# Copies between partitions by transfers, 128-row splits and a later first softmax in a decoder-layer kernel

## The chip, the cores and the metric

One core of a Trainium2 chip runs the whole layer. The metric is the device time of one execution in microseconds, the median over several runs. A profile of one execution gives the trace; its span runs from the first to the last instruction of the program.

The core has five engines with a queue of instructions each, all worked off in order: TensorE (PE in the profile, its weight loads PEld), VectorE (DVE), ScalarE (ACT), GpSimd (POOL) and SyncE (SP), which here issues all transfers.

## The reference

One decoder layer on x of 512 tokens by 1024 channels, float32. After an RMS norm, one wide projection gives a pooling branch, 16 query heads of 64, keys and values for three attention branches with two groups each, and gates. The pooling branch takes causal means over 2, 4, 8 and 16 tokens. Queries and keys get an RMS norm per head and a rotary embedding. The attention has three branches:

- compressed: keys and values are cut into 31 blocks of 32 tokens with stride 16, a position embedding is added, and each block is flattened and put through a two-layer network (gelu) to one key or value; a softmax over these blocks.
- selected: the top 8 blocks of 64 tokens, which with 512 tokens are all 8, so a causal softmax.
- window: the last 512 tokens, again a causal softmax.

```
blk  = k[:, idx] + pos_emb          # idx: 16 * n + (0..31), n = 0..30
flat = blk of one group, (n, 32 * 64)
k_cmp = gelu(flat @ w1 + b1) @ w2
s_c  = q k_cmp ;  p_c = softmax(where(16 * n + 31 <= t, s_c, -inf)) ;  o_c = p_c v_cmp
o    = g0 * o_c + g1 * o_s + g2 * o_w
```

The gated sum goes through a projection, is merged with the pooling branch by sigmoid gates, projected and added to x. Then a second RMS norm and a feed-forward part: an up projection to 2 x 2752 channels, a causal convolution over three tokens, silu(gate) * value, and a down projection, added to x.

## The kernel before

All activations lie transposed, channels on partitions, in tiles of 128 x 512. Every float32 product is computed as three products: each operand is split into a high part `hi` (a copy that rounds, on ScalarE, line 97) and a remainder `lo = x - hi` (line 100, VectorE or GpSimd), and `mm3` adds hi*hi, lo*hi and hi*lo. So every weight tile and every intermediate costs one ScalarE and one VectorE or GpSimd pass before TensorE can use it.

Weights come through `Ring` (lines 148 to 166): SyncE loads 512 KB into one of two buffers `st` (line 155), two splits of 512 columns turn it into `hi` and `lo` tiles (six of each), and the buffer is free for the next load when both splits have read it.

The stages, in the order of the program text: the first projection with the compressed keys and values and the gates (`kva`); `kv_group(0)` and `(1)` for the keys and values of the other branches; four times `pool_in`; `cmp_in`, `cmp_hid`, `cmp_out` for the compressed blocks, once for keys (i = 0) and once for values (i = 1); four times `q_group`; the attention loop; then the projections and the feed-forward part. The program is written with tile pools; a planner puts the instructions of each engine in an order by priority (the order of the text) and by the time at which its own model holds each to be ready, and it inserts the semaphores. So an instruction may stand well before or behind its place in the text, but on the chip each engine, SyncE too, keeps the planned order and waits when an operand is late.

What the change touches:

- `kcd` (lines 330 to 335): compressed keys (0) and values (1) of each block t of 128 tokens, tokens on partitions, 2 groups of 64. `cmp_in` (line 440) copies each group twice side by side into `dup` (line 450, GpSimd), transposes it on TensorE (line 451), so that partitions 0 to 63 and 64 to 127 hold the same 64 channels, and splits even tokens from the lower and odd tokens from the upper half into `X`, 64 rows at a time (line 457): eight splits for keys and eight for values.
- `kv_group` (line 338): line 311 writes the normalised key twice side by side into `k2`, 256 wide, by a broadcast; two transposes (`kt`) and a split give `KHL`.
- `q_group` (line 357): for each pair of token blocks, four transposes fill a PSUM bank `qt`; for each head half, ScalarE copies 64 rows into `qp` (line 376) and VectorE subtracts and writes the remainder into the other 64 rows of the same tile (line 377), which moves it across partitions. So a query head has its high part in one half of the rows and its low part in the other.
- `cmp_out` (line 486), called for keys and values behind two gate tiles `f_g0` (lines 549 to 552).
- the attention loop (lines 752 to 770): `u` counts 32 units (16 heads by two branches). `scores(u)` multiplies queries with keys, `soft` does maximum and exponential, `values(u - 1)` transposes the probabilities and multiplies with the values. Between them, `slot` lets pieces of gate tiles (`fm`) run on TensorE. The compressed branch is done for four heads at a time by `Cmp`: `score()` (8 products, and VectorE's mask addition `cst`), `soft()` (4 transposes `scq`, softmax), `turn()` (4 transposes back). For the first four heads `score()` and `soft()` stand ahead of `scores(0)` (ORD = 0), and `turn()` behind it.

PSUM is shared: three banks `s` (token products, scores), two banks `t` (transposes), two `g` (tiles of 512 columns), one `o`.

Of the kernel before, what the change touches and what calls it, by code (L numbers as in the profile page):

```python
# [11 lines left out]
F32 = mybir.dt.float32  # L12
F32R = mybir.dt.float32r
BF16 = mybir.dt.bfloat16
AF = mybir.ActivationFunctionType
# [4 lines left out]
P = 128  # L20
# [4 lines left out]
DH = 64  # L25
# [51 lines left out]
def layer(ctx: ExitStack, tc: tile.TileContext, par, masks, xT, w_kva, w_tm, w_fm, w_pl, w_pbr,  # L77
# [5 lines left out]
    def nm(s):  # L83
        cnt[0] += 1
        return f"{s}{cnt[0]}"
# [4 lines left out]
    def r32(ap):  # L90
        return ap.bitcast(F32)
# [193 lines left out]
    def head_norm_rope(ps, n, t, tab, out=None):  # L285

        def sc():
            return pp.tile([P, 4, DH], F32, tag="h1k", name=nm("h"), bufs=HB)  # L290
        x_, y_, z_ = sc(), sc(), sc()
        x_, y_, z_ = x_[:, :n], y_[:, :n], z_[:, :n]
        a.activation(x_, ps, AF.Copy, scale=rstd[:, t:t + 1])
        a.activation(y_, x_, AF.Square)
        ss = pp.tile([P, 4], F32, tag="hss", name=nm("hss"), bufs=4)
        v.tensor_reduce(ss[:, :n], y_, AX.X, ALU.add)
        a.activation(ss[:, :n], ss[:, :n], AF.Sqrt, bias=eps, scale=1.0 / DH)
        for h in range(2):
            s_, d_ = 32 * (1 - h), 32 * h
            g.tensor_tensor(z_[:, :, d_:d_ + 32], x_[:, :, s_:s_ + 32],  # L300
                            tabS[tab][:, t, d_:d_ + 32].unsqueeze(1).to_broadcast([P, n, 32]), ALU.mult)
        v.tensor_tensor(y_, x_, tabC[tab][:, t].unsqueeze(1).to_broadcast([P, n, DH]), ALU.mult)
        v.tensor_tensor(y_, y_, z_, ALU.add)
        rs = pp.tile([P, 4], F32, tag="hrs", name=nm("hrs"), bufs=4)
        v.reciprocal(rs[:, :n], ss[:, :n])
        rb = rs[:, :n].unsqueeze(2).to_broadcast([P, n, DH])
        if out is None:
            v.tensor_tensor(y_, y_, rb, ALU.mult)
            return y_
        o, form = out  # L310
        v.tensor_tensor(o, form(y_), form(rb), ALU.mult)
# [15 lines left out]
    heads = lambda ap: ap.rearrange("p (h d) -> p h d", d=DH)  # L327


    kcd = [[p1.tile([P, 2, DH], F32, name=f"kcd{i}{t}") for t in range(NB)] for i in range(2)]  # L330
    for t, ps in enumerate(kva):
        kr = head_norm_rope(heads(ps[:, 0:128]), 2, t, 1)
        g.tensor_copy(kcd[0][t], kr[:, 0:2])
        a.activation(kcd[1][t], heads(ps[:, 128:256]), AF.Copy, scale=rstd[:, t:t + 1])
        a.activation(gt[:, t], ps[:, 256:304], AF.Copy, scale=nrstd[:, t:t + 1])


    def kv_group(b):
        for t, ps in tok_gemm(tm_weights(b), 256):
            vin = heads(ps[:, 128:256])  # L340
            vh = V2[b][t][:, :, 0:DH]
            a.activation(vh, vin, AF.Copy, scale=rstd[:, t:t + 1])
            v.scalar_tensor_tensor(V2[b][t][:, :, DH:P], vin, rstd[:, t:t + 1], r32(vh), ALU.mult, ALU.subtract)

            k2 = pp.tile([P, 2, 2, DH], F32, tag="kq", name=nm("kd"), bufs=KQ)
            head_norm_rope(heads(ps[:, 0:128]), 2, t, 2 + b,
                           (k2, lambda x: x.unsqueeze(2).to_broadcast([P, 2, 2, DH])))
            tp = bank_t("kt")
            for G in range(2):
                pe.transpose(tp[:, G * P:(G + 1) * P], k2[:, G].rearrange("p a d -> p (a d)"), ident)  # L350
            tt = slice(t * P, (t + 1) * P)
            split(KHL[:, b, 0, :, tt], KHL[:, b, 1, :, tt], tp[:, :2 * P].rearrange("p (G q) -> p G q", q=P))
# [4 lines left out]
    def q_group(gq):  # L357
        qp = [qo.tile([P, 2, S], F32R, tag="qo", name=nm("qp"), bufs=8) for _ in range(2)]
        QP[2 * gq:2 * gq + 2] = qp
        for t, ps in tok_gemm(tm_weights(2 + gq), 256):  # L360


            q2 = pp.tile([P, 2, 2, DH], F32, tag="kq", name=nm("qd"), bufs=KQ)
            head_norm_rope(heads(ps[:, :256]), 4, t, 0,
                           (q2.rearrange("p b a d -> p a b d"),
                            lambda x: x.rearrange("p (a b) d -> p a b d", b=2)))
            if t % 2 == 0:
                tp = bank_t("qt").rearrange("p (b q) -> p b q", b=2)
            o = t % 2 * P
            for b in range(2):  # L370
                pe.transpose(tp[:, b, o:o + P], q2[:, b].rearrange("p a d -> p (a d)"), ident)
            if t % 2:
                tt = slice((t - 1) * P, (t + 1) * P)
                for a_ in range(2):
                    rh, rl = slice(64 * a_, 64 * a_ + 64), slice(64 - 64 * a_, 128 - 64 * a_)
                    a.activation(qp[a_][rh, :, tt], tp[rh], AF.Copy)
                    v.tensor_tensor(qp[a_][rl, :, tt], tp[rh], r32(qp[a_][rh, :, tt]), ALU.subtract)

    def fm_tile(ws, ht, hl_):
        ps = bank_g("fm")  # L380
# [59 lines left out]
    def cmp_in(i):  # L440
        XX = p1.tile([P, 16, 2, 2, 32], F32R, tag="X", name=nm("X"))
        Xs[i] = XX
        X = (XX[:, :, 0], XX[:, :, 1])
        g.memset(r32(XX[:, :, :, 1, 31:32]), 0.0)
        split(X[0][:, :, 0, 31], X[1][:, :, 0, 31], pv("pos")[:, 16 * i:16 * i + 16])
        for G in range(2):
            tp = bank_t("ct")
            for t in range(NB):
                dup = p1.tile([P, 2, DH], F32, tag="dup", name=nm("dup"), bufs=3)
                g.tensor_copy(dup, kcd[i][t][:, G].unsqueeze(1).to_broadcast([P, 2, DH]))  # L450
                pe.transpose(tp[:, t * P:(t + 1) * P], dup.rearrange("p a d -> p (a d)"), ident)
            for lo_ in (0, 64):
                rr = slice(lo_, lo_ + 64)
                for c in range(2):

                    src = tp[rr].rearrange("p (n f b) -> p f n b", f=8, b=2)[:, :, c:c + 31, lo_ // 64]
                    split(X[0][rr, 8 * c:8 * c + 8, G, :31], X[1][rr, 8 * c:8 * c + 8, G, :31], src)

    def cmp_hid(i):
        X = Xs[i]  # L460
# [87 lines left out]
    mp = pool(mid, "mp", side="right")  # L548
    for c in range(NPRE):
        f_g0(c, fm_tile(ring(w_fm[4 + c], P, KC), hh, hl), mp)  # L550
    cmp_out(0)
    cmp_out(1)
    mid.close()


# [194 lines left out]
    fetch(0)  # L750
    pbs = [None] * NU
    for u in range(NU + DEPTH):
        if u == ORD:
            pcs[0].score()
            pcs[0].soft()
        if u < NU:
            pbs[u] = scores(u)
        if u == max(ORD, DEPTH - 1):
            pcs[0].turn()
        w = u - DEPTH  # L760
        if w >= 0:
            values(w, pbs[w], pcs[w // 8])
            nq = w // 8 + 1
            if nq < 4:
                if w % 8 == 4:
                    pcs[nq].score()
                elif w % 8 == 5:
                    pcs[nq].soft()
                elif w % 8 == 7:
                    pcs[nq].turn()  # L770
# [195 lines left out]
```

## Time and profile before

| what | value |
|---|---|
| median of 3 runs | 843.5 us (842.94 to 844.76) |
| the profiled execution | 842.97 us |
| its span | 840.9 us |
| TensorE clock granted, mean | 0.994 |
| VectorE, ScalarE, GpSimd busy | 68%, 55%, 28% |
| HBM read | 69.94 MB |

How to read the profile: an engine's busy time is the union of its instructions. An idle stretch ahead of an instruction is given with what released it, in brackets: `[3.24 <-DVE plo L103]` means that the engine stood idle for 3.24 us until VectorE had written `plo` in line 103. PEclk is the granted share of TensorE's full clock. A line number can be a helper's: L97 and L100 are `split`, L109 to L111 `mm3`, L155 the weight load.

### The profile page before, as it was taken

What the parts mean: (1) busy time and instruction counts of PE and PEld (TensorE: products, weight loads), DVE (VectorE), ACT (ScalarE), POOL (GpSimd) and SP (SyncE); (2) the same over time, 40 slices, a digit from 0 to 9 for tenths busy, and PEclk for the clock granted to TensorE, in tenths of its full rate; (3) what the DMA queues carried; (4) which work ended last, traced back from release to release, by engine and by line L of the source; (5) the groups of instructions that cost most, each with busy time, mean ns of one, the idle gap of its engine ahead of it and who ended that gap; (6) DMA issues with size and microseconds to landing.
All of it is one profiled execution on the core that took longest, in us unless ns stands there. A gap on an engine that the chain in (4) does not pass through costs nothing.

```text
span 840.9 us, 12107 instructions
## 1 busy us (share of the span) xinstructions
PE 817.7 (97%) x4291; PEld 696.8 (83%) x4291; DVE 571.4 (68%) x1194; ACT 464.4 (55%) x985; POOL 233.7 (28%) x326
## 2 busy tenths in 40 slices
PE   7999989989999999999999999999999999999998
PEld 6888878968878878788888888888888888888888
DVE  7599976778887888886565438877777777522321
ACT  6755767757787877785334436544554454322220
POOL 5696714347575655642001200000000000000000
PEclk9999989999999999999999999999999999999999
DMA  6333132330100101011443332233332333343430
GB/s 217 103 101 113 51 101 96 107 101 25 51 26 26 51 17 35 27 39 42 135 149 112 101 103 77 101 101 101 100 91 90 97 100 116 92 128 103 113 101 26
DMA packets 23116, 72.82 MB, mean 87 GB/s; under 512 B 2832, under 2 KB 3472, under 8 KB 23056
## 3 DMA queue, kind: packets, MB, share of 16 engines
q1 hardware_dynamic: 23056, 72.05, 27.5%
q8 instruction: 34, 0.56, 0.3%
q14 instruction: 26, 0.21, 0.1%
HBM read 69.94 MB, written 2.10 MB: 86 GB/s over the span
## 4 chain that ended last, share of the span: by engine, by line
PE 85%; DVE 7%; ACT 3%; DMA 2%; issue 1%; POOL 0%; SPq 0%; ACTq 0%; DVEq 0%; POOLq 0%
PE fm L109 16%; PE fm L111 16%; PE fm L110 16%; PE op L729 5%; PE dn L109 5%; PE dn L111 5%; PE dn L110 5%; PE tp L722 4%; PE ss L691 2%; PE ss L692 2%; PE tg L321 2%; PE tg L319 2%; PE tg L320 2%; DMA st<-in_w_fm 1%; PE pb L109 1%
## 5 line engine op out<-in xcount | busy, mean ns | idle before, releaser
L97 ACT ACTIVATE hi<-st 128x512 fp32r<-128x512 f32 (+3 forms) x253 | 152.2, 607 | 189.3 <-PE fm L110 89.6
L100 DVE TENSOR_TENSOR lo<-st,hi 128x512 fp32r<-128x512 f32 (+1 forms) x210 | 145.2, 695 | 100.5 <-ACT hi L97 99.2
L109 PE MATMUL fm<-h2h,hi 128*128 128x512 f32 x344 | 134.0, 389 | 0.0
L110 PE MATMUL fm<-h2l,hi 128*128 128x512 f32 x344 | 133.8, 389 | 0.0
L111 PE MATMUL fm<-h2h,lo 128*128 128x512 f32 x344 | 133.7, 389 | 0.0
L703 POOL TENSOR_TENSOR pb<-pb,sm 128x128 f32<-128x128 f32 (+3 forms) x128 | 91.8, 748 | 49.8 <-DVE sm L700 26.1
L681 ACT ACTIVATE pb<-pb,nm 128x384 f32<-128x384 f32 (+3 forms) x128 | 70.9, 555 | 16.2 <-DVE nm L680 15.4
L111 PEld LDWEIGHTS fm<-h2h,lo 128*128 128x128 f32 x344 | 64.6, 188 | 13.5
L110 PEld LDWEIGHTS fm<-h2l,hi 128*128 128x128 f32 x344 | 64.6, 188 | 13.4
L109 PEld LDWEIGHTS fm<-h2h,hi 128*128 128x128 f32 x344 | 64.6, 188 | 13.2
L109 PE MATMUL fm<-hh,hi 128*128 128x512 f32 x160 | 71.7, 448 | 0.0
L680 DVE CUSTOM_DVE_ANT_0 pb<-ss,mk 128x384 f32<-128x384 f32 (+3 forms) x128 | 58.9, 486 | 16.7 <-PE ss L692 13.2
L110 PE MATMUL dn<-gl,hi 128*128 128x512 f32 (+1 forms) x189 | 69.1, 365 | 0.0
L111 PE MATMUL dn<-gh,lo 128*128 128x512 f32 (+1 forms) x189 | 69.1, 365 | 0.0
L109 PE MATMUL dn<-gh,hi 128*128 128x512 f32 (+1 forms) x189 | 69.1, 365 | 0.0
L111 PE MATMUL fm<-hh,lo 128*128 128x512 f32 x160 | 63.4, 397 | 0.7 <-POOL lo L100 0.7
L100 DVE TENSOR_TENSOR ptl<-tp,pth 128x512 fp32r<-128x512 f32 (+1 forms) x96 | 56.6, 594 | 10.8 <-ACT pth L97 10.2
L110 PE MATMUL fm<-hl,hi 128*128 128x512 f32 x160 | 63.4, 396 | 0.0
L97 ACT ACTIVATE pth<-tp 128x512 fp32r<-128x512 f32 (+1 forms) x96 | 49.3, 517 | 22.8 <-PE tp L722 22.5
L100 POOL TENSOR_TENSOR lo<-st,hi 128x512 fp32r<-128x512 f32 x36 | 47.2, 1313 | 41.6 <-ACT hi L97 35.6
L319 PE MATMUL tg<-hi,hh 128*128 128x256 f32 x192 | 54.4, 286 | 0.0
L320 PE MATMUL tg<-hi,hl 128*128 128x256 f32 x192 | 54.4, 286 | 0.0
(256 smaller groups left out, 1815.9 us busy)
## 6 DMA issues: line engine op xcount, KB each, us to landing
st<-in_w_up SPq DMA_DIRECT2D x43, 512.0 KB, 3.5
st<-in_w_dn SPq DMA_DIRECT2D x24, 448.0 KB, 3.4
st<-in_w_fm SPq DMA_DIRECT2D x20, 512.0 KB, 3.5
st<-in_w_tm SPq DMA_DIRECT2D x12, 512.0 KB, 3.4
st<-in_w_ab SPq DMA_DIRECT2D x8, 512.0 KB, 3.5
st<-in_w_o SPq DMA_DIRECT2D x8, 512.0 KB, 3.4
x<-in_xT SPq DMA_DIRECT2D x15, 256.0 KB, 3.7
st<-in_cw SPq DMA_DIRECT2D x4, 512.0 KB, 3.5
```

What stands on the lines that cost most here:

```text
L97: a.activation(hi, src, AF.Copy)
L100: (eng or v).tensor_tensor(lo, src, r32(hi), ALU.subtract)
L109: pe.matmul(ps, sh, mh_, start=first and i == 0, stop=False)
L110: pe.matmul(ps, sh, ml_, start=False, stop=False)
L111: pe.matmul(ps, sl, mh_, start=False, stop=last and i == n - 1)
L319: pe.matmul(ps[:, :n], hh[k][:, tt], H, start=k == 0, stop=False)
L320: pe.matmul(ps[:, :n], hl[k][:, tt], H, start=False, stop=False)
L680: v.tensor_tensor_reduce(p_, ps, mcaus[:, S - n:], -1.0, 3e38, ALU.add, ALU.min, nm_[:, i:i + 1])
L681: a.activation(p_, p_, AF.Exp, bias=nm_[:, i:i + 1], scale=-1.0, accum_out=sm[:, i:i + 1])
L703: g.tensor_tensor(pb[:, PBASE[i]:PBASE[i] + n], pb[:, PBASE[i]:PBASE[i] + n], sm[:, i:i + 1].to_broadcast([P, n]), ALU.mult)
L722: last = pe.transpose(tp[:, n:n + P], pb[:, PBASE[i] + j * P:PBASE[i] + (j + 1) * P], ident)
L729: pe.matmul(op[:, j * P:], V2[b][j][:, G], pt_[:, TBASE[j]:TBASE[j] + w], start=b == 0 and j == 0 and part == 0, stop=False)
```

## The change

The compressed keys and values go into one tile per i, `kcd[i]`, with room for two copies of each token's 64 channels: the second place of row p is to hold the token of row p + 1. For each of the four token blocks a transfer copies rows 1 to 127 one row up into the second place, and one more transfer fills row 127 from row 0 of the next blocks. GpSimd clears the second place of the last block first. `cmp_in` then transposes `kcd` directly: `dup` is gone, and since the lower half now holds token p and the upper half token p + 1, one split of 128 rows takes the even columns of both, four splits for keys and four for values.

In `kv_group`, line 311 writes `k2` once and ScalarE copies it to the second place. In `q_group` one split of 128 rows fills two new tiles `qs0` (two buffers) and `qs1` (one), and four transfers of 64 rows bring their halves into `qp`. `cmp_out(0)` moves between the two `f_g0` tiles. In the loop, `score()` of the first four heads comes behind `scores(0)`, `soft()` behind `scores(1)` and `turn()` behind `scores(2)`.

```
--- before.py
+++ after.py
@@ -327,12 +327,18 @@
     heads = lambda ap: ap.rearrange("p (h d) -> p h d", d=DH)
 
 
-    kcd = [[p1.tile([P, 2, DH], F32, name=f"kcd{i}{t}") for t in range(NB)] for i in range(2)]
+
+    kcd = [p1.tile([P, NB, 2, 2, DH], F32, name=f"kcd{i}") for i in range(2)]
+    for i in range(2):
+        g.memset(kcd[i][:, NB - 1, :, 1], 0.0)
     for t, ps in enumerate(kva):
-        kr = head_norm_rope(heads(ps[:, 0:128]), 2, t, 1)
-        g.tensor_copy(kcd[0][t], kr[:, 0:2])
-        a.activation(kcd[1][t], heads(ps[:, 128:256]), AF.Copy, scale=rstd[:, t:t + 1])
+        head_norm_rope(heads(ps[:, 0:128]), 2, t, 1, (kcd[0][:, t, :, 0], lambda x: x))
+        a.activation(kcd[1][:, t, :, 0], heads(ps[:, 128:256]), AF.Copy, scale=rstd[:, t:t + 1])
         a.activation(gt[:, t], ps[:, 256:304], AF.Copy, scale=nrstd[:, t:t + 1])
+    for k_ in kcd:
+        for t in range(NB):
+            nc.sync.dma_start(k_[:P - 1, t, :, 1], k_[1:, t, :, 0])
+        nc.sync.dma_start(k_[P - 1:, :NB - 1, :, 1], k_[:1, 1:, :, 0])
 
 
     def kv_group(b):
@@ -343,8 +349,8 @@
             v.scalar_tensor_tensor(V2[b][t][:, :, DH:P], vin, rstd[:, t:t + 1], r32(vh), ALU.mult, ALU.subtract)
 
             k2 = pp.tile([P, 2, 2, DH], F32, tag="kq", name=nm("kd"), bufs=KQ)
-            head_norm_rope(heads(ps[:, 0:128]), 2, t, 2 + b,
-                           (k2, lambda x: x.unsqueeze(2).to_broadcast([P, 2, 2, DH])))
+            head_norm_rope(heads(ps[:, 0:128]), 2, t, 2 + b, (k2[:, :, 0], lambda x: x))
+            a.activation(k2[:, :, 1], k2[:, :, 0], AF.Copy)
             tp = bank_t("kt")
             for G in range(2):
                 pe.transpose(tp[:, G * P:(G + 1) * P], k2[:, G].rearrange("p a d -> p (a d)"), ident)
@@ -371,10 +377,13 @@
                 pe.transpose(tp[:, b, o:o + P], q2[:, b].rearrange("p a d -> p (a d)"), ident)
             if t % 2:
                 tt = slice((t - 1) * P, (t + 1) * P)
+                qs = [pp.tile([P, 2, 2 * P], F32R, tag=f"qs{j}", name=nm("qs"), bufs=2 - j) for j in range(2)]
+                split(qs[0], qs[1], tp)
                 for a_ in range(2):
-                    rh, rl = slice(64 * a_, 64 * a_ + 64), slice(64 - 64 * a_, 128 - 64 * a_)
-                    a.activation(qp[a_][rh, :, tt], tp[rh], AF.Copy)
-                    v.tensor_tensor(qp[a_][rl, :, tt], tp[rh], r32(qp[a_][rh, :, tt]), ALU.subtract)
+                    rh = slice(64 * a_, 64 * a_ + 64)
+                    for j in range(2):
+                        ro = slice(64 * (a_ ^ j), 64 * (a_ ^ j) + 64)
+                        nc.sync.dma_start(r32(qp[a_][ro, :, tt]), r32(qs[j][rh]))
 
     def fm_tile(ws, ht, hl_):
         ps = bank_g("fm")
@@ -446,15 +455,11 @@
         for G in range(2):
             tp = bank_t("ct")
             for t in range(NB):
-                dup = p1.tile([P, 2, DH], F32, tag="dup", name=nm("dup"), bufs=3)
-                g.tensor_copy(dup, kcd[i][t][:, G].unsqueeze(1).to_broadcast([P, 2, DH]))
-                pe.transpose(tp[:, t * P:(t + 1) * P], dup.rearrange("p a d -> p (a d)"), ident)
-            for lo_ in (0, 64):
-                rr = slice(lo_, lo_ + 64)
-                for c in range(2):
-
-                    src = tp[rr].rearrange("p (n f b) -> p f n b", f=8, b=2)[:, :, c:c + 31, lo_ // 64]
-                    split(X[0][rr, 8 * c:8 * c + 8, G, :31], X[1][rr, 8 * c:8 * c + 8, G, :31], src)
+                pe.transpose(tp[:, t * P:(t + 1) * P], kcd[i][:, t, G].rearrange("p a d -> p (a d)"), ident)
+            for c in range(2):
+
+                src = tp.rearrange("p (n f b) -> p f n b", f=8, b=2)[:, :, c:c + 31, 0]
+                split(X[0][:, 8 * c:8 * c + 8, G, :31], X[1][:, 8 * c:8 * c + 8, G, :31], src)
 
     def cmp_hid(i):
         X = Xs[i]
@@ -548,8 +553,7 @@
     mp = pool(mid, "mp", side="right")
     for c in range(NPRE):
         f_g0(c, fm_tile(ring(w_fm[4 + c], P, KC), hh, hl), mp)
-    cmp_out(0)
-    cmp_out(1)
+        cmp_out(c)
     mid.close()
 
 
@@ -750,12 +754,13 @@
     fetch(0)
     pbs = [None] * NU
     for u in range(NU + DEPTH):
-        if u == ORD:
-            pcs[0].score()
-            pcs[0].soft()
         if u < NU:
             pbs[u] = scores(u)
-        if u == max(ORD, DEPTH - 1):
+        if u == 0:
+            pcs[0].score()
+        if u == 1:
+            pcs[0].soft()
+        if u == 2:
             pcs[0].turn()
         w = u - DEPTH
         if w >= 0:
```

## Rows read from the trace of the kernel before

**Rows 1.** The page's busy times: us, share of the span, instructions of each engine.

```profile
PE 817.7 (97%) x4291; PEld 696.8 (83%) x4291; DVE 571.4 (68%) x1194; ACT 464.4 (55%) x985; POOL 233.7 (28%) x326
```

**Rows 2.** Busy time by stretch: length, then each engine, PEclk, DMA share, GB/s.

```profile
60.00:80.00 20.00, 18.20 (x147) 17.48 (x146) 19.24 (x37) 10.70 (x29) 14.94 (x23) 1.00 0.28 79
...
100.00:115.00 15.00, 10.54 (x56) 9.07 (x55) 14.34 (x28) 12.06 (x26) 5.05 (x8) 0.77 0.33 96
115.00:176.00 61.00, 61.00 (x377) 53.97 (x376) 42.81 (x98) 42.60 (x90) 22.08 (x33) 1.00 0.31 98
176.00:187.00 11.00, 7.61 (x33) 6.10 (x33) 7.44 (x19) 5.50 (x15) 2.55 (x2) 0.84 0.33 95
```

**Rows 3.** The same view in windows of 2 us, for PEclk (third number from the end).

```profile
108.00:110.00 2.00, 1.55 (x7) 1.55 (x8) 1.91 (x4) 0.94 (x3) 0.00 (x0) 0.50 0.61 225
112.00:114.00 2.00, 2.00 (x12) 2.00 (x11) 1.94 (x4) 1.75 (x6) 0.15 (x1) 0.53 0.28 43
182.00:184.00 2.00, 2.00 (x9) 1.81 (x10) 1.59 (x8) 0.38 (x2) 0.00 (x0) 0.54 0.45 184
184.00:186.00 2.00, 2.00 (x8) 1.61 (x7) 0.67 (x3) 1.39 (x5) 0.00 (x0) 0.61 0.00 0
```

**Rows 4.** Timeline of PE and DVE: start, length, engine, line, operands, count.

```profile
108.45 0.79 PE L473 MATMUL hp<-hi,X 128*128 128x256 f32 x2 [3.24 <-DVE plo L103]
...
181.15 0.69 DVE L624 TENSOR_TENSOR cst<-sc,mk 128x512 f32<-128x512 f32 x1
...
181.89 0.90 PE L629 MATMUL scq<-pk,cst 128*128 128x128 f32 x4 [3.39 <-DVE cst L624]
```

**Rows 5.** Groups by line and shape: count, busy us, mean ns, idle before (qp: 80 to 115).

```profile
L377 DVE TENSOR_TENSOR qp<-qt,qp 64x512 fp32r<-64x512 f32 x5 | 3.4, 688 | 0.3 <-ACT qp L376 0.2
...
L100 DVE TENSOR_TENSOR X<-ct,X 64x248 fp32r<-64x248 f32 x16 | 6.6, 413 | 4.0 <-ACT X L97 3.8
L311 DVE TENSOR_TENSOR kd<-h,hrs 128x256 f32<-128x256 f32 x8 | 6.0, 760 | 0.1
...
L450 POOL COPY dup<-kcd 128x128 f32<-128x128 f32 x16 | 5.6, 375 | 10.6 <-PE ct L451 10.6
...
L100 DVE TENSOR_TENSOR KHL<-kt,KHL 128x256 fp32r<-128x256 f32 x8 | 3.2, 410 | 0.0
```

**Rows 6.** Timeline of ACT and DVE: first value copy and last key of `kcd`.

```profile
31.36 0.39 ACT L334 ACTIVATE kcd<-raw,rstd 128x128 f32<-128x128 f32 x1
...
45.71 0.29 DVE L308 TENSOR_TENSOR h<-h,hrs 128x128 f32<-128x128 f32 x1
```

**Rows 7.** Transfers of the span: packets; queue's share; issues, KB, us to landing.

```profile
DMA packets 23116, 72.82 MB, mean 87 GB/s; under 512 B 2832, under 2 KB 3472, under 8 KB 23056
...
q1 hardware_dynamic: 23056, 72.05, 27.5%
...
out<-o SPq DMA_DIRECT2D x2, 128.0 KB, 1.9
...
w<-in_cw SPq DMA_DIRECT2D x2, 32.0 KB, 4.2
```

**Rows 8.** Timeline of SyncE's queue: two weight loads, start and length of the issue.

```profile
49.71 0.33 SPq L155 DMA_DIRECT2D st<-in_w_tm  x1
...
106.59 0.33 SPq L155 DMA_DIRECT2D st<-in_w_tm  x1
```

**Rows 9.** Transfers in the window 13.9 to 14.1 us.

```profile
DMA packets 30, 0.01 MB, mean 31 GB/s; under 512 B 30, under 2 KB 30, under 8 KB 30
...
q1 hardware_dynamic: 30, 0.01, 15.2%
```

**Rows 10.** Timeline of PE where `kv_group(1)` begins.

```profile
57.60 0.39 PE L110 MATMUL fm<-hl,hi 128*128 128x512 f32 x1
57.83 0.28 PE L319 MATMUL tg<-hi,hh 128*128 128x256 f32 x1
```

**Rows 11.** Timeline of PE, the first transposes of `cmp_in`.

```profile
87.29 0.49 PE L451 MATMUL ct<-pk,dup 128*128 128x128 f32 x3
```

## The prediction

> **What bounds the kernel now.** Read the page's engine shares first: TensorE is busy for 97% of the span [rows 1]. So time can be won only where TensorE stands idle or runs at the lower of its two clocks, and is lost where a new wait stops it. Next the stretches [rows 2]: from 115 to 176 us TensorE is busy throughout, and three stretches leave something. From 60 to 80 it idles 20.0 - 18.2 = 1.8 us; from 100 to 115, 4.5; from 176 to 187, 3.4. VectorE tells why in the first two: it is busy 19.2 of 20 and 14.3 of 15 us, so TensorE has run ahead of its evictions.
>
> Third, short windows for the clock [rows 3] with the timeline beside them [rows 4]. After the 3.24 us idle before `hp` (line 473) the granted clock is 0.50, the 1.2 GHz level, from 108 until about 113; after the 3.39 us idle before `scq` (line 629) it is about half from 182 to somewhat before 186. Work done at half speed could have been done in half the time, so the dips cost about 4.8/2 = 2.4 and 3.5/2 = 1.75 us. The prize is 4.5 + 2.4 = 6.9 us at 100 to 115 (place A), 3.4 + 1.75 = 5.1 at 176 to 187 (place B), 1.8 at 60 to 80 (place C): 13.8 us at most.
>
> **The change part by part: what it takes away.** First, whether 128 rows cost more than 64. They don't: VectorE's subtraction takes 413 ns on 64x248 (`X`) and 410 on 128x256 (`KHL`) [rows 5]. So half the count is half the time.
>
> `cmp_in`: 16 subtractions of 413 ns become 8, saving 3.3 us of VectorE (half of it before 115 us) and about as much of ScalarE. The 16 `dup` copies at 375 ns leave GpSimd, 6.0 us. `q_group`: 16 subtractions of 688 ns become 8; five of the 16 lie before 115, so 2.5 x 0.69 = 1.7 us goes there. `kv_group`: the multiplication of line 311 becomes 128 wide instead of 256; its eight take a mean of 760 ns against 290 for an undisturbed 128-wide one [rows 5, 6], at best 3.8 us, by the undisturbed 410 ns of a 256-wide operation 1.0; I take 2. ScalarE gets eight 128-wide copies instead, 0.39 us each by the `kcd` row [rows 6]; it has room (10.7 busy of 20 us at 60 to 80 [rows 2]), but every `kt` transpose waits one hop longer.
>
> VectorE thus loses about 1.7 + 1.7 + 2 = 5.4 us of its work before 115, more than the 4.5 us of idle at A. I credit 5 of A's 6.9 us (in-order engines keep a remainder) and all 1.8 of C. Bounds for both: 2.2 (only the two `q_group` and two `cmp_in` subtractions next to the stalled `plo` splits, 2 x 0.69 + 2 x 0.41) and 8.7.
>
> The loop's start: at B, TensorE has issued `sc`, and its next instruction, the `scq` transposes, waits for `cst`, which VectorE reaches only at 181.15, behind older work [rows 4]. After the change `scores(0)` stands ahead of `score()`: its products need only `KHL` and `QP[0]`, and behind each of its four blocks come two pieces of an `fm` tile: 4 x 2 x 3 products of 512 columns, 0.23 us apart [rows 10], 5.5 us of work that waits for nothing on VectorE. That covers the 3.4 us. I credit 4.5 of 5.1 (bounds 3.4 and 5.1): `soft()` and `turn()` now crowd VectorE among the first units. `cmp_out(0)` ahead of `f_g0(1)` I cost at nothing: TensorE is solid there.
>
> Credit: 5 + 1.8 + 4.5 = 11.3 us, bounds 5.6 and 13.8.
>
> **What it adds.** SyncE gets 10 transfers for `kcd` and 32 for `qp`. A `qp` copy is 128 KB; the nearest row lands in 1.9 us [rows 7], and SyncE issues a transfer in 0.33 us, four in 1.3 [rows 8]. Nobody reads `qp` before the attention, and two token blocks lie between pairs, 48 products of 256 columns at half of the 0.23 us that one of 512 takes [rows 10], 5.5 us, so the single `qs1` is free again by then. I take 0.5 us for weight loads that stand behind them; bounds 0 and 9 (second rival).
>
> The `kcd` copies decide. Each of eight moves 127 rows of two pieces of 256 B, 254 pieces. What does a piece cost? The trace holds no copy within the chip, but it holds the loads of `w2`, 128 pieces of 256 B each [rows 7]. In a window in which only such small packets move, 30 of them take 15.2% of 16 engines for 0.2 us: 0.486/30 = 16 ns each [rows 9]. From the other sides: by bytes alone, 72.05 MB in 27.5% of 16 x 840.9 us, 256 B take 13 ns; the mean packet, 12 times larger, takes 160 ns [rows 7]. I take 16, the row of the same size.
>
> How many of the 16 DMA engines share the pieces? In this kernel every transfer has 128 or 64 rows, which divide by 16, and the page shows how they are dealt: of 2832 packets under 512 B [rows 7], 256 are the `w2` rows; the other 2576 are 16 x 161, and 161 is the number of transfers in the list of issues: one closing packet from each engine for each. 127 is prime: it can't be dealt in equal shares to 16 engines, nor to any number but one. So there are two cases: one engine, 254 x 16 ns = 4.1 us a copy, or all sixteen, 0.26 us and nothing to notice. I take one engine, since every share in the trace is an equal one.
>
> The Trainium skill says this outright ("DMA: Bandwidth & Descriptors", section "Why a DMA increments its semaphore by 16 and not by 1"): a hardware-queued transfer runs on the largest number of engines up to 16 that divides the slowest dimension of both its sides, and 127 rows is its example of a transfer that gets one. The 16 closing packets agree for 128 and 64 rows; no run here shows 127. By that rule the sum is the one below, without it the first rival's.
>
> With one engine: the first `kcd[1]` copy is ready at 31.36 + 0.39 = 31.75 (line 334), the last `kcd[0]` one at 46.0 (line 308) [rows 6]. The first can move data from about 31.75 + 1.9 = 33.6 on; the eight follow each other, to 33.6 + 8 x 4.1 = 66.4. Weight loads go out on the same queue in SyncE's order and use all 16 engines, so their sixteenth on that engine waits. Behind the copies come the `w_fm` load of `pool_in(3)` and the first `w_tm` load of `kv_group(1)`, issued at 49.71 [rows 8]; each adds 8 packets of 160 ns, 1.3 us, so the second lands at 69.0. With 0.6 for ScalarE's cast TensorE starts `kv_group(1)` at 69.6 where it started at 57.83 [rows 10]: 11.8 us late, with nothing else to do in its order. The wait comes in two gaps (before `pool_in(3)` and before `kv_group(1)`), each likely over 3 us, so I add the two measured dips, 2.4 + 1.75 = 4.2. Cost 16.0 us. At 13 ns it is 5.6 late with half the dips, about 8; at 20 ns 19.9 and 4.2, about 24. The `ct` transposes, which read the copies, come at 87.29 [rows 11], so that wait is covered; late are the weights behind the copies.
>
> **Sum.** 842.97 (the profiled execution) - 11.3 + 0.5 + 16.0 = 848.2. The runs' median lies 0.5 above the profiled one: 848.7.
>
> **Rivals.** First, faster: the 127 rows are dealt over all engines, or the planner puts the copies behind the weight loads. Then a copy is 2 us of latency that nobody reads before 87 us, and the credit stays: 843.5 - 11.3 + 0.5 = 832.7. For it: SyncE is busy for 0.33 us per load only; against it: the equal shares. It decides from where the eight copies are done before the `w_tm` load of 49.71, at 2 us a copy or less.
>
> Second, no change: without one engine, the transfers' place in SyncE's in-order queue eats the credit. A weight load behind four `qp` copies waits for the split that they wait for (0.7) and for four issues (1.3); another 0.3 for their packets. The load issued at 106.59 [rows 8], just before the `q_group` work at 113, stands so. Four such places, 9.2 us: 842. Against it: the loads wait for the same VectorE anyway.
>
> Third, much slower: a piece within the chip costs 25% more than one from memory, 20 ns, or the queue stops SyncE too: 857 and above.
>
> **How the numbers follow.** Chances: forecast 0.58, first rival 0.27, second 0.08, third 0.07. Within 0.2% (1.7 us) counts as the same, about what a measurement of this kernel tells from no change. The forecast's own range is 840 to 857, from 13 to 20 ns; since its credit and its cost are both larger than their difference, I give 0.42 of its 0.58 to slower, 0.08 to the same, 0.08 to faster. First rival: 0.25 faster, 0.02 the same. Second: 0.03 the same, 0.02 faster, 0.03 slower. Third: slower. Sums: faster 0.35, same 0.13, slower 0.52. The range reaches over the first rival and leaves out a tenth on either side: 831 to 857.
>
> **What would show it.** One engine: fewer than 16 closing packets a transfer, `kcd` copies that land 4 us apart, the `w_tm` load issued near 50 landing late, and a TensorE gap that ends on a weight split between 52 and 70 us. Credit: no gap over 1 us before `hp`, none before `scq`, and a clock of 1.00 there. If TensorE runs through 50 to 70 us as before, the forecast is wrong and the first rival holds; if the gaps at A and B remain, the credit is.

## The result: 1.5 per cent slower, and the profile after

The changed kernel takes 856.66 us (median of 4 runs, 856.32 to 857.26) against 843.43 for the kernel before: ratio 1.0154, 95% interval 1.0142 to 1.0166. That is 13.2 us more, where the forecast's sum has 5.2. The profiled execution has a span of 854.4 us.

The page's own lines, those that answer to [rows 1, 7]:

```profile
PE 820.4 (96%) x4291; PEld 699.4 (82%) x4291; DVE 557.9 (65%) x1178; ACT 456.7 (53%) x977; POOL 226.8 (27%) x308
...
DMA packets 29790, 77.55 MB, mean 91 GB/s; under 512 B 5409, under 2 KB 10145, under 8 KB 29729
...
q1 hardware_dynamic: 29728, 76.77, 30.2%
```

VectorE, ScalarE and GpSimd all do less, 13.5, 7.7 and 6.9 us, and the kernel is slower: their sums say nothing of the end. The stretches do (columns as in [rows 2]):

```profile
40.00:60.00 20.00, 11.49 (x61) 9.25 (x60) 11.12 (x29) 5.06 (x16) 9.89 (x17) 0.87 0.08 16
60.00:80.00 20.00, 13.24 (x58) 11.07 (x59) 11.93 (x23) 8.54 (x22) 10.54 (x13) 0.71 0.42 126
...
100.00:120.00 20.00, 20.00 (x162) 19.42 (x161) 16.73 (x40) 14.02 (x36) 10.35 (x17) 1.00 0.42 107
120.00:140.00 20.00, 17.69 (x88) 14.40 (x87) 13.99 (x36) 12.76 (x29) 2.76 (x5) 0.91 0.65 184
...
208.00:222.00 14.00, 10.34 (x53) 8.24 (x52) 8.67 (x28) 7.21 (x20) 8.87 (x11) 0.88 0.00 1
```

From 40 to 80 us TensorE is busy for 24.7 of 40 us and no other engine for more; such a hole in all of them at once points at a transfer. SyncE's queue (start, us, engine, line, operands, count; lines 340 and 341 are the `kcd` copies, 155 the weight loads) shows which. Before, the last `w_fm` load of the early stages went out like this:

```profile
43.45 0.33 SPq L155 DMA_DIRECT2D st<-in_w_fm  x1
```

In the changed kernel, some lines left out:

```profile
36.38 8.35 SPq L340 DMA_DIRECT2D kcd<-kcd  x2
44.77 4.14 SPq L341 DMA_DIRECT2D kcd<-kcd  x1
48.96 8.36 SPq L340 DMA_DIRECT2D kcd<-kcd  x3
57.42 4.05 SPq L155 DMA_DIRECT2D st<-in_w_fm  x1
...
67.17 1.76 SPq L155 DMA_DIRECT2D st<-in_w_tm  x2
```

An issue of a weight load took 0.33 us before. Of the eleven issues from 32 to 67 us (ten copies and the `w_fm` load), eight hold SyncE for 3.3 to 4.8 us each and three for under 1 us. So the `w_fm` load goes out at 57.42 instead of 43.45, and the `w_tm` load of 49.71 [rows 8] at 67.17. While only copies move, the transfers of the window 40 to 44 us are

```profile
DMA packets 244, 0.06 MB, mean 16 GB/s; under 512 B 244, under 2 KB 244, under 8 KB 244
...
q1 hardware_dynamic: 244, 0.06, 7.9%
```

244 pieces in 4 us are one every 16.4 ns. 7.9% of sixteen engines is 1.3 engines, so by engine time a piece takes 20.7 ns: each begins a little before the one ahead of it is done. ScalarE and TensorE then wait in one chain (timeline; in brackets the idle time before and what ended it):

```profile
65.36 1.15 ACT L97 ACTIVATE hi<-st 128x512 fp32r<-128x512 f32 x2 [15.82 <-DMA st<-in_w_fm]
...
66.76 0.69 PE L356 MATMUL kt<-pk,kd 128*128 128x128 f32 x2 [14.60 <-ACT kd L353]
```

`kt` waits for ScalarE's copy of `kd`, which stands behind the cast of the late weights. So it is one gap of 14.60 us, and the half clock after it (0.50 from 60 to 70, 0.83 from 70 to 75) costs about 2.5 more.

At the loop's start the wait before `scq` [rows 4] is gone, and there is this in the changed kernel:

```profile
210.53 0.17 DVE L643 TENSOR_TENSOR csm<-csm,gt 128x16 f32<-128x16 f32 x1
210.69 2.75 POOL L707 TENSOR_TENSOR pb<-pb,sm 128x128 f32<-128x128 f32 x4 [1.58 <-DVE csm L643]
...
213.40 1.05 POOL L646 TENSOR_TENSOR ce<-ce,csm 128x512 f32<-128x512 f32 x1
...
214.50 0.66 PE L652 MATMUL pct<-pk,ce 128*128 128x128 f32 x4 [3.29 <-POOL ce L646]
```

The `pct` transposes wait for `ce`, which in GpSimd's order stands behind four multiplications of the next unit. 3.29 us and a clock of 0.88 over 14 us: the wait that went, in another place.

Two marks on TensorE divide the 13.5 us by which the two profiled spans differ. The 17th `hp` product, the first of the second `cmp_hid`, starts at 150.04 before and 162.59 after, 12.6 later; the 200th `op` product, well inside the attention, at 346.60 and 360.01, 13.4 later; from there on the distance stays.

### The profile page after: what moved, and what is told of

Its sections match the earlier page's. It is cut to its first block, busy times and chain, and to the rows that moved or that the text cites. A ratio compares the mean times of both kernels' runs of the same rounds, so it can differ in the third digit from the quotient of the medians.

```text
span 854.4 us, 12146 instructions
## 1 busy us (share of the span) xinstructions
PE 820.4 (96%) x4291; PEld 699.4 (82%) x4291; DVE 557.9 (65%) x1178; ACT 456.7 (53%) x977; POOL 226.8 (27%) x308
## 4 chain that ended last, share of the span: by engine, by line
PE 80%; DVE 8%; DMA 4%; ACT 3%; issue 2%; POOL 2%; SPq 1%; DVEq 0%; ACTq 0%; POOLq 0%
PE fm L109 15%; PE fm L111 15%; PE fm L110 15%; PE dn L111 4%; PE dn L109 4%; PE dn L110 4%; PE op L733 4%; PE tp L726 4%; DMA st<-in_w_fm 2%; PE ss L695 2%; PE ss L696 2%; PE tg L321 1%; PE tg L320 1%; PE tg L319 1%; PE pb L109 1%
## 5 line engine op out<-in xcount | busy, mean ns | idle before, releaser
L100 DVE TENSOR_TENSOR lo<-st,hi 128x512 fp32r<-128x512 f32 (+1 forms) x210 | 142.9, 685 | 108.7 <-ACT hi L97 107.8
L685 ACT ACTIVATE pb<-pb,nm 128x384 f32<-128x384 f32 (+3 forms) x128 | 70.9, 555 | 14.2 <-DVE nm L684 13.5
L111 PEld LDWEIGHTS fm<-h2h,lo 128*128 128x128 f32 x344 | 64.6, 188 | 13.5
L109 PEld LDWEIGHTS fm<-h2h,hi 128*128 128x128 f32 x344 | 64.6, 188 | 13.4
```

What stands on the lines that cost most here:

```text
L100: (eng or v).tensor_tensor(lo, src, r32(hi), ALU.subtract)
L109: pe.matmul(ps, sh, mh_, start=first and i == 0, stop=False)
L111: pe.matmul(ps, sl, mh_, start=False, stop=last and i == n - 1)
L685: a.activation(p_, p_, AF.Exp, bias=nm_[:, i:i + 1], scale=-1.0, accum_out=sm[:, i:i + 1])
```

## The experiments

Fifteen kernels; each ratio is to runs of the kernel before on the same chip (medians 843.2 to 843.8), with its 95% interval.

**The copies, dealt over all engines.** In the changed kernel:

```diff
-            nc.sync.dma_start(k_[:P - 1, t, :, 1], k_[1:, t, :, 0])
+            for r0, r1 in ((0, 112), (112, P - 1)):
+                nc.sync.dma_start(k_[r0:r1, t, :, 1], k_[r0 + 1:r1 + 1, t, :, 0])
```

> The changed kernel, but each 127-row copy of kcd is made by two transfers of 112 and 15 rows (16 and 15 equal shares). Theory (127 rows go through one DMA engine, 4.2 us a copy, and hold the weight loads): the 14.6 us gap of TensorE at 52 to 67 us and the half clock behind it go, 856.7 - 16 = 840.5 us (838 to 843), no SyncE issue over 1 us there. Rival (copies within the chip or their number in SyncE's queue are slow however they are dealt): 10 transfers more make it no better, 855 or above.

Measured: 841.70 us, ratio 0.9974 (0.9959 to 0.9989). The same bytes in more transfers take 15.0 us off. TensorE's waits for ScalarE's `kd` (us in total, times, the longest), in the changed kernel and then here:

```profile
PE kt L356 <- ACT kd L353: 15.7, 2, 14.6
```

```profile
PE kt L357 <- ACT kd L354: 2.7, 2, 1.8
```

The gap is gone. Shown: the number of rows in a transfer made it.

**What a copy of n rows takes by itself.** In the kernel before, one copy every second unit of the attention, into a tile that is written only later:

```diff
+    rows = {4 + 2 * i: n for i, n in enumerate((128, 127, 126, 125, 124, 122, 120, 112, 127, 128))}
     for u in range(NU + DEPTH):
...
+        if u in rows:
+            n = rows[u]
+            o = min(1, P - n)
+            nc.sync.dma_start(lad[:n, :, 1], lad[o:o + n, :, 0])
```

> The kernel before, with ten copies within the chip added during the attention, some 24 us apart, each of n rows of two pieces of 256 B that nobody reads; n = 128, 127, 126, 125, 124, 122, 120, 112, 127, 128. If the rows are dealt in equal shares over the largest number of engines up to 16 that divides n (16, 1, 14, 5, 4, 2, 15, 16, 1, 16), then at 16 ns a piece the pieces take 0.26, 4.1, 0.29, 0.8, 1.0, 2.0, 0.26, 0.22, 4.1, 0.26 us beyond a common start of some 2 us. If only odd or prime counts go to one engine, 126, 124, 122 and 120 land alike and as early as 128. If the copies are slow for another reason (the shift by one partition), 126 to 112 land as late as 127. The time of the whole kernel should not change: nobody waits for them.

The planner drew the ten copies together, each issued when the one before had landed. The transfers of five windows, each from one copy's issue to the next one's, for 127, 126, 125, 124 and 112 rows:

```profile
DMA packets 255, 0.07 MB, mean 11 GB/s; under 512 B 255, under 2 KB 255, under 8 KB 255
...
DMA packets 266, 0.06 MB, mean 27 GB/s; under 512 B 266, under 2 KB 266, under 8 KB 266
...
DMA packets 255, 0.06 MB, mean 24 GB/s; under 512 B 255, under 2 KB 255, under 8 KB 255
...
DMA packets 252, 0.06 MB, mean 23 GB/s; under 512 B 252, under 2 KB 252, under 8 KB 252
...
DMA packets 240, 0.06 MB, mean 27 GB/s; under 512 B 240, under 2 KB 240, under 8 KB 240
```

Two pieces a row leave 1, 14, 5, 4 and 16 closing packets, one for each engine that took part: the largest divisor of n up to 16. This is the rule of the Trainium skill ("DMA: Bandwidth & Descriptors", section "Why a DMA increments its semaphore by 16 and not by 1"), and here the trace agrees with it count by count. From issue to issue it is 5.95 and 6.02 us for 127 rows, then 2.36, 2.70, 2.78 and 2.13. One engine has 254 pieces where each of sixteen has 14, and 240 x 16 ns is 3.84, the difference of 127 and 112. The second theory of the expectation falls, since 125 rows, odd, run on five engines; so does the third, since 126 rows are shifted too. The one timed execution, 845.07, lies inside the spread of the kernel before (841.7 to 845.2).

**Who stands: the queue or the engine?** The changed kernel with its ten copies issued by ScalarE:

```diff
-            nc.sync.dma_start(k_[:P - 1, t, :, 1], k_[1:, t, :, 0])
-        nc.sync.dma_start(k_[P - 1:, :NB - 1, :, 1], k_[:1, 1:, :, 0])
+            nc.scalar.dma_start(k_[:P - 1, t, :, 1], k_[1:, t, :, 0])
+        nc.scalar.dma_start(k_[P - 1:, :NB - 1, :, 1], k_[:1, 1:, :, 0])
```

> The changed kernel (856.7 us) with its ten kcd copies, 127 rows as they are, issued by ScalarE's queue instead of SyncE's. If the weight loads were late because SyncE itself stood in its issues, each 4.2 us after the other, they go out in time now: 843 to 846 if ScalarE doesn't stand likewise, and 860 or more if it does (its casts then wait 4 us behind each issue). If they were late because a sixteenth of each lies on the one engine that the copies fill, they stay late: 853 to 857.

Measured: 861.48 us, ratio 1.0217 (1.0203 to 1.0231). ScalarE's timeline in it (ACTq is its queue of transfers):

```profile
36.63 8.34 ACTq L340 DMA_DIRECT2D kcd<-kcd  x2
45.02 0.29 ACT L297 ACTIVATE hss<-hss,eps 128x2 f32<-128x2 f32 x1 [9.79 <-issue]
```

ScalarE computes nothing for 9.79 us, ended by "issue": two issues hold it for 8.34 us, about as long as two copies take. TensorE waits 11.88 us for ScalarE's cast of `hi` (at 52.02). The one DMA engine makes a copy long; the standing issuer carries it to everything behind.

Does a weight load beside such copies also wait for its share on their engine, as the prediction had it? This run can't say, but the ladder's trace can. There a `w_fm` load went out at 199.52, 0.8 us behind the copy of 122 rows, which two engines share. The packets from 202.70 to 203.02 us, then those from 203.70 to 203.80:

```profile
DMA packets 29, 0.06 MB, mean 192 GB/s; under 512 B 14, under 2 KB 14, under 8 KB 29
```

```profile
DMA packets 2, 0.00 MB, mean 0 GB/s; under 512 B 2, under 2 KB 2, under 8 KB 2
```

Fourteen of the load's closing packets come by 203.02, the last two, as many as the copy has engines, some 0.7 us later, and it lands 4.7 us after its issue instead of 3.4. So both happen: the issuer stands, and a load's share waits on the engines that a copy fills. How they divide the gap of 14.60 us is not shown.

**The loop's start, undone, alone, and undone with whole-engine copies.** The edit between the kernels is the last part of the change's diff.

> The changed kernel with the start of the attention loop as before (score and soft ahead of scores(0), turn behind it). Theory (the loop's edit only moved TensorE's wait from scq to pct, 3.4 us against 3.3): 855 us (854 to 857.5), the 3.4 us gap before scq back, no gap before pct. Rival (the edit is worth the 4.5 us that was credited, and something else lost them): 861.

> Both edits: copies of 112 and 15 rows, loop start as before. Theory: the two effects add, 839 to 840 us; what then remains against before (843.4) is the credit of the splits at 100 to 115 us, about 4. Rival (the splits are worth nothing, all of it was the loop's): 843.

> The kernel before with only the new start of the attention's loop (scores(0) first, then score(), soft() after scores(1), turn() after scores(2)). By the forecast's term B: 843.8 - 4.5 = 839.3. By what the changed kernel's trace shows, the wait before scq (3.4 us) goes and one before pct, behind GpSimd's multiplications of scores(1), comes in its place with the half clock after it: 844 to 847. If the new gap only comes with the other edits, 840.

Measured: the changed kernel with the old start 853.49 us, ratio 1.0115 (1.0093 to 1.0136), 3.2 less than with the new one; the same with 112 + 15 rows 839.52, 0.9944 (0.9927 to 0.9961), 2.2 less than the first experiment; the new start alone on the kernel before 845.95, 1.0032 (1.0021 to 1.0043), 2.3 more. Three pairs, one sign: the new order costs 2 to 3 us where a win of 4.5 was forecast. In the first two TensorE waits before `scq` (2.32 and 2.67 us), in the third before `pct`. The second and the third:

```profile
178.12 0.66 PE L634 MATMUL scq<-pk,cst 128*128 128x128 f32 x4 [2.67 <-DVE cst L629]
```

```profile
203.34 0.86 PE L648 MATMUL pct<-pk,ce 128*128 128x128 f32 x4 [3.30 <-POOL ce L642]
```

The marks agree: from the one to the other it is 197.4 us in the changed kernel, 195.3 in the same with the old start, and 196.6 in the kernel before.

**Is it GpSimd's order?** Two edits of the first experiment: `ce` of the first four heads on VectorE, and `soft()` one step earlier, which puts `ce` ahead of the multiplications.

```diff
-            g.tensor_tensor(e, e, smb, ALU.mult)
+            (v if self.h0 == 0 else g).tensor_tensor(e, e, smb, ALU.mult)
```

> Copies of 112 and 15 rows, the changed loop start, and the multiplication of e by the row factors for the first four heads on VectorE instead of GpSimd. Theory (pct waits for ce because ce stands behind four pb multiplications of 2.75 us in GpSimd's order): the 3.3 us gap before pct shrinks under 1 us and its half clock goes, 4 us less than the copies of 112 and 15 rows alone, 836.5 (835 to 838.5). Rival (the softmax chain on VectorE is itself that late): within 1 us of them.

```diff
             pcs[0].score()
-        if u == 1:
             pcs[0].soft()
```

> As the first run (copies in 112 + 15 rows, the changed loop, 841.7 us), but soft() is called right after score(), one step earlier: GpSimd's multiplication ce then stands ahead of the four of scores(1) instead of behind them, and scq is the transposes after score() with nothing between. If GpSimd's order makes the pct wait (3.29 us and a dip), it goes: 838 to 839 with a smaller wait before scq (under 2 us, as scores(0) gives VectorE time). If the softmax chain on VectorE is itself the last, the wait stays as in the fourth run or moves to scq: 840.5 to 842.

Measured: 840.56 us, ratio 0.9956 (0.9936 to 0.9976), and 841.84, 0.9976 (0.9963 to 0.9989), against 841.70 without them. My theory of GpSimd's order falls as a cause of the time. In the former the `pct` wait shrinks to 1.15 us and one before `ss` grows from 0.62 to 1.16. In the latter it is gone, and TensorE waits here instead (timeline of that kernel, of the slowest of its twelve executions, which spread from 838.70 to 843.77):

```profile
183.14 0.47 PE L696 MATMUL ss<-KHL,qp 128*128 128x512 f32 x1 [1.39 <-DVE nm L685]
...
189.17 0.33 PE L727 MATMUL tp<-pk,pb 128*128 128x128 f32 x1 [2.11 <-POOL pb L708]
```

Each order names another operand that comes last. So the theory became: what TensorE lacks there is work that waits for nothing.

**Work in place of order.** Eight pieces of an `fm` tile (5.5 us of products) between `score()` and `soft()`, the old order otherwise; the pieces behind are spread a little more thinly. First on the kernel with 112 + 15 rows and the old start, then on the kernel before:

```diff
-            pcs[0].score()
+            slot(8, pcs[0].score())      # score() returns its last product
             pcs[0].soft()
```

> As the third run (112 + 15 rows, the loop's start as before, 839.5 us), with eight pieces of an fm tile (8 x 3 products of 512 columns, 5.5 us) between score() and the scq transposes; the other pieces are spread more thinly over the units behind. If what TensorE lacks at the loop's start is work that waits for nothing, the wait before scq (2.67 us) and its half clock go and nothing comes in their place: 836. If the wait only moves on again, as it did to pct, 839 to 841: the chain of VectorE and GpSimd, not the order, sets the start, or the later units miss their pieces.

> The kernel before with nothing changed but the eight pieces of an fm tile between score() and the scq transposes. If the idle at the loop's start is a prize of its own (the ninth run won 4 us with it on top of the third), 839.5 us, with no wait before scq and none before pct. If the nine run's gain needs the earlier VectorE of the other edits, the wait before scq stays in part, or moves to ss: 841.5 to 843.

Measured: 835.57 us, ratio 0.9900 (0.9884 to 0.9915), and 838.48, 0.9936 (0.9923 to 0.9950): 4.0 and 5.3 us won, about the whole prize of place B (5.1). In the traces 3.0 and 4.0 of it lie between the two marks. The stretch from 170 to 200 us in the kernel without the pieces (the old start with 112 + 15 rows) and then with them:

```profile
170.00:200.00 30.00, 26.91 (x134) 21.76 (x133) 20.59 (x60) 18.82 (x50) 16.94 (x19) 0.94 0.29 87
```

```profile
170.00:200.00 30.00, 29.18 (x145) 23.50 (x144) 22.01 (x60) 19.36 (x48) 18.99 (x20) 1.00 0.40 114
```

TensorE is busy 2.3 us more and its clock stays at 1.00; nothing came in the wait's place but 0.67 us before `ss`.

**The early stages, part by part.** On the kernel before, `q_group`'s part alone and the part of the compressed keys and values (`kcd`) alone (112 + 15 rows), both as in the change's diff; and the kernel with 112 + 15 rows and the old start, with `k2` written by VectorE as before.

> The kernel before with q_group's part alone: one pair of 128-row splits for a pair of blocks and four transfers of 64 rows, 32 in all. By the forecast, VectorE and ScalarE lose 2.5 x 0.69 = 1.7 us before 115 us, and the queue costs 0.5: 842.4. If SyncE's queue holds up the weight loads behind the transfers (second rival), 844 to 850. If this part carries most of the 4.1 us that the third run won, 840.

> The kernel before with the compressed keys' part alone, its copies in 112 + 15 rows: no dup copies, 8 + 8 splits of 128 rows instead of 16 + 16 of 64. By the forecast VectorE loses 1.7 us before 115 us and GpSimd 6: 841.5 to 842. If this part carries most of the 4.1 us that the third run won, 840; if the 18 small transfers cost as much as the splits give, 843.6.

> The copies in 112 + 15 rows, the loop's start as before (as the third run, 839.5 us), and in kv_group the key tile k2 written once for both halves by VectorE's 256-wide multiplication, as before, so that ScalarE's eight copies of k2 are gone. Theory of place C: the hop over ScalarE holds up each kt transpose, so the kt gap of 1.76 us at 76 us goes and VectorE's wider multiplications (+0.1 us each undisturbed) cost less than that: 838 us. Rival: VectorE is what the stretch waits for, its eight wider multiplications (1 to 3 us) come back at the q_group gaps: 840 to 842.

Measured: `q_group` alone 844.29 us, ratio 1.0006 (0.9996 to 1.0016); `kcd` alone 845.39, 1.0014 (1.0003 to 1.0024); `k2` as before 840.46 us, 0.9963 (0.9949 to 0.9977), 0.9 more than with ScalarE's copies, with overlapping intervals. Neither part wins alone, and all together won 4.3 (839.52). The move of `cmp_out(0)`, which is in the whole and in neither part, was not timed by itself; it stands where TensorE is busy throughout (55.00 of 55 us from 120 to 175 in the whole). The traces show what stood in the way of each part. With `q_group` alone the wait before `hp` [rows 4] is gone, but TensorE waits 2.62 us before `qt` for VectorE's split of `qs` and 3.74 us at 113.17 for this cast of weights:

```profile
112.49 1.15 ACT L97 ACTIVATE hi<-st 128x512 fp32r<-128x512 f32 x2 [3.52 <-DMA st<-in_w_tm]
```

and the transfers from 104 to 113 us are

```profile
q1 hardware_dynamic: 1203, 2.09, 89.8%
...
st<-in_w_tm SPq DMA_DIRECT2D x2, 512.0 KB, 5.8
qp<-qs SPq DMA_DIRECT2D x6, 128.0 KB, 5.7
```

The sixteen engines are 90% busy, with 1 KB pieces of `qp` and with weights. The two `w_tm` loads issued there land in 5.8 us (median) instead of 3.5, though the first, issued at 106.15, went out no later than before [rows 8]. With the `kcd` part alone TensorE waits at the next place for VectorE:

```profile
113.54 0.27 PE L482 MATMUL ht<-pk,hs 64*128 64x64 f32 x1 [2.72 <-DVE hs L480]
```

**SyncE's queue, once more.** In the kernels with 18 copies in it TensorE has new waits before 80 us. The expectations below put them at some 3 us between 50 and 60; that was a wrong reading. With 112 + 15 rows and either start TensorE idles 1.3 us there (8.7 of 10 us busy, 10.0 before), and 4.1 from 40 to 80 us, where it was 2.5 before. With the eight pieces above, one copy of 112 rows and one of 15 for a whole tensor (6 issues), on SyncE and then on ScalarE:

```diff
-        for t in range(NB):
-            for r0, r1 in ((0, 112), (112, P - 1)):
-                nc.sync.dma_start(k_[r0:r1, t, :, 1], k_[r0 + 1:r1 + 1, t, :, 0])
+        for r0, r1 in ((0, 112), (112, P - 1)):
+            nc.sync.dma_start(k_[r0:r1, :, :, 1], k_[r0 + 1:r1 + 1, :, :, 0])
```

> As the ninth run (835.6 us), but the eight copies in 112 + 15 rows are merged to one of 112 and one of 15 rows for each of the two tensors, eight pieces a row instead of two: 6 issues on SyncE instead of 18. In the kernels with 18 issues the w_fm load of pool_in(3) goes out at about 50.2 us instead of 43.45, and TensorE loses some 3 us between 50 and 60. If the number of issues in SyncE's queue is the cause, the load goes out before 47 and most of the 3 us come back: 833. If the wait of the second tensor's copies for the last key, at 47 us or so, is the cause, the loads behind it stay late: 835 to 836.

> As the thirteenth run, with the six copies issued by ScalarE instead of SyncE, so that no weight load stands behind a copy. If SyncE's queue is what costs the 3 us between 50 and 60 us, the loads go out as before the change (43.45, 49.71) and the time is 832.5; ScalarE's six issues of 0.7 us and its wait for the last key may give back about 1. If the 3 us come from elsewhere (VectorE's new order), 835.6 as the ninth run.

Measured: 835.45 us, ratio 0.9910 (0.9897 to 0.9924), and 837.68, 0.9926 (0.9913 to 0.9940): 835.57 without the edit, so nothing is won, and with the issues on ScalarE it takes 2 us more. In the former the `w_fm` load goes out nearly as before, and the waits moved on to `kt`:

```profile
44.16 0.35 SPq L155 DMA_DIRECT2D st<-in_w_fm  x1
```

```profile
75.05 0.47 PE L356 MATMUL kt<-pk,kd 128*128 128x128 f32 x1 [2.06 <-ACT kd L353]
```

The queue was late, but it wasn't what held the time: with it in time, nothing is won, and 3.6 us from 40 to 80 are still idle. From 50 to 58 us VectorE is busy 7.97 of 8 us in that kernel. ScalarE's copy of `k2` alone doesn't make the `kt` waits either: with `k2` as before 4.1 us are idle from 40 to 80. They come with the `kcd` part: alone on the kernel before it leaves 4.1 us idle there, `q_group`'s part alone 2.4. What in that part makes them, the order that VectorE gets or something else, stays open.

The 835.57 and 835.45 us kernels beat both others and are equal to each other within their spread: 21 us below the changed kernel, 8 below the one before.

## Why the forecast was too small

**The copies: right in cause, the size partly by luck.** One engine, 4.1 us a copy and 16.0 us in all were forecast. Measured: 4.1 to 4.2 us a copy, and 15.0 us between the changed kernel and the first experiment. The terms inside differ. The forecast has 11.8 us of delay in two gaps and 4.2 of clock; the trace has one gap of 14.60, since ScalarE's copy of `kd`, queued behind the late cast, held up the `kt` transposes too, and 2.5 of clock. Of these 17.1 us 15.0 were won back, since the first experiment's kernel has the waits of place C in their stead. `kv_group(1)` began at 78.26 and not at 69.6, behind 11 us of `fm` products that the gap had held up. The 16 ns is a meeting of two measures: [rows 9] gives a packet's mean engine time, and six of its thirty are closing packets (9 ns each, the 24 pieces of 256 B 18 ns). By engine time a piece of the copies takes 20.7 ns, but what sets a copy's length is that one follows the other every 16.4. So both conditions of the third rival show, 20 ns and a SyncE that stands, and yet the cost came out near the forecast's.

**Place B: the failed step.** "I credit 4.5 of 5.1" was wrong in sign: three pairs of runs give a loss of 2.2 to 3.2. The reason given, 5.5 us of work that waits for nothing, was true of the wait before `scq`, which did go. What the step left out is the end of the same chain: `soft()` and `turn()` moved behind further units, and the work of these stands ahead of theirs. In the changed kernel it is GpSimd's multiplications ahead of `ce`; in the two kernels that took `ce` out from behind them it was other operands, for much the same time. I named VectorE's crowding and took 0.6 us for it, and did not follow the chain to its last reader, `pct`. The prize itself was sized right: with extra work in place of a new order it is 4.0 to 5.3 us.

**Place C: wrong in sign; place A: nearly right.** 5 + 1.8 - 0.5 = 6.3 us were credited for the early stages; with 112 + 15 rows and the old start 4.3 were won. The stretches of that kernel (columns as in [rows 2]) say where:

```profile
40.00:60.00 20.00, 18.01 (x94) 14.67 (x95) 18.86 (x44) 10.94 (x33) 16.48 (x26) 1.00 0.22 66
60.00:80.00 20.00, 17.91 (x129) 16.67 (x128) 14.82 (x32) 10.05 (x26) 12.42 (x23) 1.00 0.36 119
...
100.00:120.00 20.00, 17.76 (x109) 15.27 (x108) 16.36 (x41) 14.34 (x35) 5.57 (x9) 1.00 0.71 173
```

From 100 to 120 us 2.2 us of idle are left of A's 4.5, and the clock stays at 1.00: 4.7 of 6.9 us won, where 5 were credited. In the changed kernel less is won: a clock of 0.91 and 2.3 us of idle remain from 120 to 140, before `qt`, `ct` and `ht`. From 40 to 80 us TensorE idles 4.1 us, where the kernel before idled 2.5 (in these stretches 19.32 and 18.20 us busy of 20): where all 1.8 us were credited, 1.6 were lost. Before `scq` the wait is 0.7 us shorter (2.67 for 3.39), which makes 3.8 in all; the profiled spans differ by 3.6. The waits stand before `kt` (0.94, 0.35 and 1.76 us). I had said that every `kt` waits one hop longer and had not priced it, but the waits come with the `kcd` part, which the sum charges with late weights alone. The parts don't add: with either alone another operand is last. The second rival's late load did appear in one run, beside the `qp` copies, but by shared DMA engines and not by SyncE's order.

**The sum.** Copies 15.0 instead of 16.0, place B +2.2 instead of -4.5, the early stages -4.3 instead of -6.3: 12.9, where 13.2 were measured. These three are steps from the kernel before to the one with 112 + 15 rows and the old start, from there to the first experiment's and to the changed one, so they must add up; they show where the microseconds lie. Of the 8 us missed, about 7 are place B, and 2 the early stages, less 1 of the copies.

## What to carry to other kernels

Count the rows of a transfer before its bytes: the closing packets in the profile tell how many engines share it, and 112 + 15 rows did in this kernel what 127 could not. At the loop's start here the idle stretch was closed by work that waits for nothing, and not by a new order: before crediting a reordering, follow the moved chain to its last reader and list what then stands ahead of it on each engine. Savings in several parts of one busy stretch are to be timed apart and together, for here they didn't add, and a part that saves work on every engine can still bring TensorE new waits.

## What was not expected of the hardware

An engine that issues transfers can stand in the issue itself: with copies that one DMA engine works off, eight of eleven issues held SyncE for 3.3 to 4.8 us, and ScalarE did nothing for 9.79 us. A load beside a copy on two engines had two of its sixteen closing packets 0.7 us late. Pieces of 256 B from one partition to another followed each other every 16.4 ns on one engine, at 20.7 ns of engine time each. And transfers of 1 KB pieces, 128 KB each, kept the sixteen engines 90% busy together with the weights, and two weight loads beside them took 5.8 us instead of 3.5.
